# GLA's values by token: two token tiles at a time, placed by transfers within SBUF

## The chip, the cores and the metric

The kernel runs on one core of a Trainium2 chip. The metric is device time in microseconds (us) of one execution, and the median over runs is what is compared. The engines are TensorE (PE, and PEld for its weight loads), VectorE (DVE), ScalarE (ACT), GpSimd (POOL) and SyncE (SP, which here only issues transfers). Each engine works through its own list of instructions in order and waits on semaphores of the others.

## The reference

A two-layer trunk for 512 tokens of width 1024. Layer 0 has one input projection, whose columns feed gated linear attention (GLA, 4 heads, key width 64, value width 128, chunks of 64 tokens) and an RWKV-7 mixer (8 heads of 64); then an output projection, a LayerNorm and a SwiGLU feed-forward. Layer 1 is a latent attention with 16 heads, and another feed-forward. The part that the change touches is the GLA values `v`:

```python
p = x @ w_in                                  # (512 tokens) x (columns)
gq, gk, gv, gg, glr = jnp.split(p_gla, GLA_OFFSETS, axis=-1)
# per chunk of 64 tokens and head, S the state (64 x 128):
o_inter = einsum('bhck,bhkv->bhcv', qi * exp(b), state)
o_intra = einsum('bhij,bhjv->bhiv', attn, vi)
new_state = exp(b_last) * state + einsum('bhck,bhcv->bhkv', ki * exp(b_last - b), vi)
```

Both products take a chunk's values with the 64 tokens on the partitions and the 128 value columns along the free axis.

## The kernel before

Every large product is done in three passes over float32 split in two parts: a rounded part h and a rest l (`gemm3`, lines 184 to 187: three matmuls of 512 columns that accumulate in one PSUM bank). The input x stands in SBUF transposed, as `xh` and `xl` (128 partitions, 8 blocks of 128 rows of x, 512 tokens).

**Weights of layer 0's input projection.** `w_even` lies in HBM as 27 tiles of 128 columns, each with 1024 floats per partition (8 blocks k of 128 columns). `half_w(..., add=True)` (lines 207 to 219) brings half of such a tile, 128 x 512 floats, 256 KB, with 2 KB per partition in one piece:

1. SP issues the transfer into `w` (line 212).
2. ACT writes -w into `wl` (line 214).
3. POOL issues a second transfer of the same weights, which adds them in float32 onto `wl` (line 215); so `wl` becomes what rounding takes away.
4. ACT casts `w` to `wh` (line 216).

`w`, `wh` and `wl` have three buffers each, so a fourth load waits until the first one's products are done. `proj(i)` (lines 251 to 260) takes two such halves for one tile of 128 columns and does 24 matmuls, 12 for each half, with the weights as the stationary side; its result has the columns on the partitions and the tokens along the free axis. The results go to two PSUM banks with the tag "g".

**The values before.** Tiles 19 to 22 are the four heads' values. `plain` (line 830) runs `proj` for each and copies the result to `gv`, column by token. `gla_states` (line 877), for each of the two pairs of heads i, needs them token by column. So `turn` (line 886) multiplies each 128 x 64 piece with the identity: as a matmul for one head (line 891) and as a transpose for the other (line 889), four chunks of both heads into the one PSUM bank with the tag "l"; ACT and DVE copy that bank to `SV` (line 913). There are four such rounds (2 pairs x 2 halves of the chunks). The keys `ke` are turned in the same way ahead of it. Line 919 forms the keys' and values' products, line 927 the states, and `gla_out` (line 955) the outputs.

**The order.** `weave` interleaves the streams (the projections "0 1 2 k 3 v g", four RWKV heads' pairs, GLA, the output projection) by costs in the program, and the framework's scheduler then sets the final order on every engine. So between a projection's products stand small products of the RWKV and GLA streams: lines 870 (GLA scores), 674 and 694 (inversion), 715 (chunk products, 64 x 64), 562, 520. The pool "S2" has 14 buffers of 128 x 512 floats; the `SV` tiles come from it and take those that RWKV's third pair of heads gives back.

Of the kernel before, what the change touches and what calls it, by code (L numbers as in the profile page):

```python
# [17 lines left out]
P = 128  # L18
# [3 lines left out]
CH = 64  # L22
# [184 lines left out]
def half_w(g, src, tag=None, add=False):  # L207

    nc = g.nc
    w = g.tp.tile([P, 512], F32, tag="w", name="w", bufs=3)  # L210
    h, l = (g.T(tag, n, dt=F32R) if tag else g.tp.tile([P, 512], F32R, tag=n, name=n, bufs=3) for n in ("wh", "wl"))
    nc.sync.dma_start(w, src)
    if add:
        nc.scalar.mul(l, w, -1.0)  # L214
        nc.gpsimd.dma_start(l, src, accum_op=ALU.add)  # L215
    nc.scalar.copy(h, w)  # L216
    if not add:
        nc.gpsimd.tensor_tensor(l, in0=w, in1=h, op=ALU.subtract)
    return h, l
# [6 lines left out]
def even_mixer(g, xh, xl, big, big2):  # L226
# [145 lines left out]
            yield from rproj(int(o))  # L372
        done.add("proj")

    gla = gla_projections(g, L, proj, done)

    def rwkv(i):
        while ("r", i) not in done or i > 2 and f"o{i - 3}" not in done:
# [434 lines left out]
    return L  # L813


def gla_projections(g, L, proj, done):
    nc = g.nc
    T = g.T
    g.v, g.gate = [], []

    def keys():
        for i, e in enumerate(L):
            e.q, e.k = T("L", "gq"), T("L", "gk")
            nc.scalar.mul(e.q, proj(15 + 2 * i), 0.125)
            yield 5 * g.slow
            nc.scalar.copy(e.k, proj(16 + 2 * i))
            yield 5 * g.slow
        done.add("gk")

    def plain(dst, c, name):  # L830
        for i in range(4):
            t = T("L" if name == "gv" else "S1", name)
            nc.scalar.copy(t, proj(c + i))
            dst.append(t)
            yield 5 * g.slow
        done.add(name)

    return {"k": keys(), "v": plain(g.v, 19, "gv"), "g": plain(g.gate, 23, "gg")}


def gla_scores(g, L):
# [35 lines left out]
def gla_states(g, L):  # L877


    nc = g.nc  # L880
    C, T, ps = g.C, g.T, g.ps
    ch = lambda t: t.rearrange("p (c t) -> p c t", t=CH)
    hs = [slice(0, 64), slice(64, 128)]
    g.QA, g.SV = [], []

    def turn(h, o, i, one):

        if h:
            nc.tensor.transpose(out=o, in_=i, identity=one)
        else:  # L890
            nc.tensor.matmul(o, lhsT=i, rhs=one, start=True, stop=True)  # L891

    for i, e in enumerate(L):
        ke = T("v", "ke")
        nc.vector.tensor_tensor(ch(ke), in0=bc(ch(e.b)[:, :, CH - 1:CH], [P, NCH, CH]), in1=ch(e.b), op=ALU.subtract)
        exp_ln(g, ke, ke, AF.Exp, scale=1.0 / 16)
        nc.vector.tensor_tensor(ke, in0=ke, in1=e.k, op=ALU.mult)
        p = ps("l")
        for c in range(NCH):
            for h in range(2):  # L900
                turn(h, p[hs[1 - h], c * CH:(c + 1) * CH], ke[hs[h], c * CH:(c + 1) * CH], C("ident")[hs[h], hs[h]])
        kt = T("v", "kt", (P, NCH, CH))
        nc.scalar.copy(kt.rearrange("p c t -> p (c t)"), p)
        yield 4
        SV = [[T("S2", "SV", (P, 4, P)) for r in range(2)] for h in range(2)]
        g.SV += SV
        for r in range(2):
            p = ps("l")
            for j in range(4):
                for h in range(2):  # L910
                    turn(h, p[hs[1 - h], j * P:(j + 1) * P], g.v[2 * i + h][:, (4 * r + j) * CH:(4 * r + j + 1) * CH], C("ident"))
            for h in range(2):
                (nc.vector.tensor_copy if h else nc.scalar.copy)(SV[h][r][hs[1 - h]], p[hs[1 - h]].rearrange("p (c v) -> p c v", v=P))
            yield 3
        for r in range(2):
            o = ps("l")
            for c in range(4 * r, min(4 * r + 4, NCH - 1)):
                for h in range(2):
                    nc.tensor.matmul(o[hs[h], c % 4 * P:c % 4 * P + P], lhsT=kt[hs[1 - h], c], rhs=SV[h][r][hs[1 - h], c % 4], start=True, stop=True)
            for c in range(4 * r, min(4 * r + 4, NCH - 1)):  # L920
                for h in range(2):
                    st, nx, kv = SV[h][r][hs[h], c % 4], SV[h][(c + 1) // 4][hs[h], (c + 1) % 4], o[hs[h], c % 4 * P:c % 4 * P + P]
                    if c == 0:
                        nc.gpsimd.memset(st, 0.0)
                        nc.scalar.copy(nx, kv)
                    else:
                        nc.vector.scalar_tensor_tensor(nx, in0=st, scalar=e.el[hs[h], c:c + 1], in1=kv, op0=ALU.mult, op1=ALU.add)
            yield 3
        qe = T("v", "qe")
        exp_ln(g, qe, e.b, AF.Exp, scale=1.0 / 16)  # L930
        for h in range(2):
            qa = T("S2", "QA", (P, NCH, CH))
            g.QA.append(qa)
            nc.gpsimd.tensor_tensor(qa.rearrange("p c t -> p (c t)")[hs[h]], in0=qe[hs[h]], in1=e.q[hs[h]], op=ALU.mult)
            nc.gpsimd.tensor_copy(qa[hs[1 - h]].rearrange("p c t -> p (c t)"), g.acc[i][hs[1 - h]])
        yield 2
# [886 lines left out]
```

## Time and profile before

| | us |
|---|---|
| median of 3 runs | 1387.27 |
| lowest and highest | 1384.99 and 1394.15 |
| the profiled execution | 1391.69 |
| its span, first to last instruction | 1389.6 |
| PE busy in the span | 1342.3 (97%) |

The page gives the busy time of each engine, the chain that ended last and groups of instructions by line; the trace can be asked for a stretch, a line, or the instructions in order of time. Matmuls overlap in the records: one of 512 columns is shown as 390 ns and the next starts 230 ns after it. So what a matmul takes of PE's time is read from the starts. The granted clock of TensorE stands as a share of 2.4 GHz: 1.00 is 2.4 GHz and 0.50 is 1.2 GHz.

### The profile page before, as it was taken

What the parts mean: (1) busy time and instruction counts of PE and PEld (TensorE: products, weight loads), DVE (VectorE), ACT (ScalarE), POOL (GpSimd) and SP (SyncE); (2) the same over time, 40 slices, a digit from 0 to 9 for tenths busy, and PEclk for the clock granted to TensorE, in tenths of its full rate; (3) what the DMA queues carried; (4) which work ended last, traced back from release to release, by engine and by line L of the source; (5) the groups of instructions that cost most, each with busy time, mean ns of one, the idle gap of its engine ahead of it and who ended that gap; (6) DMA issues with size and microseconds to landing.
All of it is one profiled execution on the core that took longest, in us unless ns stands there. A gap on an engine that the chain in (4) does not pass through costs nothing.

```text
span 1389.6 us, 21744 instructions
## 1 busy us (share of the span) xinstructions
PE 1342.3 (97%) x8382; PEld 1063.7 (77%) x8382; DVE 921.3 (66%) x1704; ACT 685.1 (49%) x1212; POOL 232.6 (17%) x278
## 2 busy tenths in 40 slices
PE   8899999999999899999999999999999899999997
PEld 6577777766678688998888877666677788997886
DVE  3687677644497666668456367988786766667456
ACT  6653344354536455555334356555445455555341
POOL 2230012122311111126401130000011111120000
PEclk9999999979999999999999999999999999999999
DMA  8563343530468788673325422111277787773232
GB/s 244 111 128 59 70 100 68 113 67 32 157 214 191 163 186 166 149 141 84 103 96 149 118 79 58 55 56 46 92 206 172 161 187 167 145 127 93 91 107 90
DMA packets 74328, 168.15 MB, mean 121 GB/s; under 512 B 21232, under 2 KB 22384, under 8 KB 74096
## 3 DMA queue, kind: packets, MB, share of 16 engines
q0 software_dynamic: 21888, 60.83, 26.2%
q1 hardware_dynamic: 51808, 103.83, 22.9%
q10 hardware_dynamic: 528, 2.10, 0.4%
q8 instruction: 66, 1.08, 0.3%
q14 instruction: 38, 0.31, 0.1%
HBM read 163.77 MB, written 2.95 MB: 120 GB/s over the span
## 4 chain that ended last, share of the span: by engine, by line
PE 62%; issue 14%; DMA 10%; DVE 7%; ACT 3%; POOL 2%; SPq 1%; POOLq 0%; DVEq 0%; ACTq 0%
PE ps_g L1239 12%; PE ps_g L186 10%; PE ps_g L187 10%; PE ps_g L185 10%; DMA raw<-in_w_gu 6%; PE ps_s L1624 3%; PE ps_o L1653 2%; PE ps_c L715 2%; PE ps_t L1640 1%; POOL raw L1266 1%; PE ps_c L674 1%; DMA wl<-in_w_even 1%; PE ps_l L891 1%; PE ps_s L1317 1%; PE ps_c L187 1%
## 5 line engine op out<-in xcount | busy, mean ns | idle before, releaser
L192 DVE TENSOR_TENSOR wl<-raw,wh 128x1024 fp32r<-128x1024 f32 (+1 forms) x120 | 132.7, 1114 | 80.2 <-ACT wh L191 79.8
L191 ACT CAST wh<-raw 128x1024 fp32r<-128x1024 f32 (+1 forms) x120 | 116.0, 968 | 138.2 <-PE ps_g L1239 101.1
L1266 POOL DMA_DIRECT2D raw<-in_w_gu x96 | 83.1, 866 | 494.3 <-DVE wl L192 388.5
L1239 PE MATMUL ps_g<-wh,xh 128*128 128x512 f32 (+1 forms) x320 | 118.9, 372 | 2.0 <-ACT wh L191 2.0
L1239 PE MATMUL ps_g<-wh,xl 128*128 128x512 f32 (+1 forms) x320 | 117.8, 368 | 0.0
L187 PE MATMUL ps_g<-xh,wl 128*128 128x512 f32 (+2 forms) x296 | 113.7, 385 | 3.0 <-DMA wl<-in_w_even 1.8
L185 PE MATMUL ps_g<-xh,wh 128*128 128x512 f32 (+2 forms) x296 | 115.6, 391 | 0.0
L186 PE MATMUL ps_g<-xl,wh 128*128 128x512 f32 (+2 forms) x296 | 114.1, 385 | 0.0
L186 PE MATMUL ps_g<-wl,ah 128*128 128x512 f32 x288 | 112.0, 390 | 0.6 <-DVE wl L192 0.6
L185 PE MATMUL ps_g<-wh,ah 128*128 128x512 f32 x288 | 111.7, 392 | 0.6 <-ACT ah L191 0.4
L187 PE MATMUL ps_g<-wh,al 128*128 128x512 f32 x288 | 110.8, 389 | 0.0
L192 DVE TENSOR_TENSOR wl<-w,wh 128x1024 fp32r<-128x1024 f32 (+2 forms) x79 | 89.4, 1131 | 32.0 <-ACT wh L191 31.6
L191 ACT CAST wh<-w 128x1024 fp32r<-128x1024 f32 (+2 forms) x79 | 76.2, 965 | 60.2 <-PE ps_g L186 36.6
L191 ACT CAST ah<-hid 128x512 fp32r<-128x512 f32 x72 | 43.5, 618 | 98.9 <-PE ps_g L186 98.9
L1239 PE MATMUL ps_g<-wh,Sh 128*128 128x512 f32 (+1 forms) x240 | 90.1, 376 | 0.0
L192 DVE TENSOR_TENSOR al<-hid,ah 128x512 fp32r<-128x512 f32 x72 | 49.2, 695 | 60.9 <-ACT ah L191 60.8
L1239 PE MATMUL ps_g<-wh,Sl 128*128 128x512 f32 (+1 forms) x240 | 89.3, 373 | 0.0
L1239 PE MATMUL ps_g<-wl,xh 128*128 128x512 f32 (+1 forms) x320 | 79.7, 371 | 0.9 <-DVE wl L192 0.9
L215 POOL DMA_DIRECT2D wl<-in_w_even x48 | 41.5, 865 | 229.9 <-ACT wl L214 194.8
L216 ACT CAST wh<-w 128x512 fp32r<-128x512 f32 x64 | 39.3, 617 | 81.5 <-PE ps_g L186 49.7
L1239 PEld LDWEIGHTS ps_g<-wh,xh 128*128 128x128 f32 x320 | 60.1, 188 | 10.5 <-ACT wh L191 2.9
L187 PEld LDWEIGHTS ps_g<-xh,wl 128*128 128x128 f32 (+1 forms) x296 | 56.2, 190 | 14.7 <-DMA wl<-in_w_even 3.0
(461 smaller groups left out, 3269.4 us busy)
## 6 DMA issues: line engine op xcount, KB each, us to landing
raw<-in_w_gu POOLq DMA_DIRECT2D x64, 512.0 KB, 5.7
w<-in_w_dn SPq DMA_DIRECT2D x44, 512.0 KB
raw<-in_w_gu SPq DMA_DIRECT2D x32, 512.0 KB
w<-in_w_even SPq DMA_DIRECT2D x48, 256.0 KB
wl<-in_w_even POOLq DMA_DIRECT2D x48, 256.0 KB, 4.7
raw<-in_w_gu POOLq DMA_DIRECT2D x32, 384.0 KB, 4.8
w<-in_w_gu SPq DMA_DIRECT2D x12, 512.0 KB
raw<-in_w_gu SPq DMA_DIRECT2D x16, 384.0 KB
```

The lines of the kernel that those rows point to most:

```text
L185: nc.tensor.matmul(out, lhsT=wh, rhs=xh, start=first, stop=False)
L186: nc.tensor.matmul(out, lhsT=wh, rhs=xl, start=False, stop=False)
L187: nc.tensor.matmul(out, lhsT=wl, rhs=xh, start=False, stop=last)
L191: c = nc.scalar.copy(h, src)
L192: (eng or nc.vector).tensor_tensor(l, in0=src, in1=h, op=ALU.subtract)
L215: nc.gpsimd.dma_start(l, src, accum_op=ALU.add)
L216: nc.scalar.copy(h, w)
L715: nc.tensor.matmul(q[:, CH:] if m else q[:, :CH], lhsT=l, rhs=r, start=m < 2, stop=m != 1)
L1239: nc.tensor.matmul(acc[u][:, :n], lhsT=A_[a][:, k, P * u:P * u + P], rhs=w[:, q], start=first and k + a + b == 0, stop=k + b == 4, skip_gr ...
L1266: nc.gpsimd.dma_start(T[k][k2], w[r, q, k2], accum_op=ALU.add)
L1624: nc.tensor.matmul(p[:, :nk], lhsT=Q[:, h % 4, qb * P:(qb + 1) * P], rhs=K[:, h % 4, :nk], start=True, stop=True)
L1653: nc.tensor.matmul(o[64 * e:64 * e + 64, kb * P:], lhsT=Vv[:, kb, (h - 1 + e) * 64:(h + e) * 64], rhs=t[e][kb][:, kb * P:], start=kb == 0, ...
```

## The change

The values are computed with the tokens on the partitions: the stationary side is now a block of x (128 tokens), the moving side the weights of all four heads, 512 columns. One load brings block k of the four tiles 19 to 22, that is 4 pieces of 512 bytes per partition, which lie 512 KB apart in HBM. Two tiles of tokens are done at a time, in both "g" banks, so each load serves 6 matmuls, and all loads are made twice (two halves of the tokens). The turning products, their bank and their copies are gone; 32 transfers issued by SP, each 64 partitions x 512 bytes, put the values from `gv` into `SV`.

```diff
@@ half_w
+    as_src = lambda t: t.rearrange("p (i c) -> p i c", c=P) if len(src.shape) == 3 else t
-    nc.sync.dma_start(w, src)
+    nc.sync.dma_start(as_src(w), src)
     if add:
         nc.scalar.mul(l, w, -1.0)
-        nc.gpsimd.dma_start(l, src, accum_op=ALU.add)
+        nc.gpsimd.dma_start(as_src(l), src, accum_op=ALU.add)
@@ gla_projections
+    def values():
+
+        for half in range(2):
+            o = [g.ps("g") for u in range(2)]
+            for k in range(NK):
+                h, l = half_w(g, g.I["w_even"][19:23, :, k * P:k * P + P].transpose([1, 0, 2]), add=True)
+                for u in range(2):
+                    ts_ = slice((2 * half + u) * P, (2 * half + u) * P + P)
+                    gemm3(nc, o[u], xh[:, k, ts_], xl[:, k, ts_], h, l, k == 0, k == NK - 1)
+            for u in range(2):
+                g.v.append(T("L", "gv"))
+                nc.scalar.copy(g.v[-1], o[u])
+            yield 10 * g.slow
+        done.add("gv")
+
-    return {"k": keys(), "v": plain(g.v, 19, "gv"), "g": plain(g.gate, 23, "gg")}
+    return {"k": keys(), "v": values(), "g": plain(g.gate, 23, "gg")}
@@ gla_states
-        for r in range(2):
-            p = ps("l")
-            for j in range(4):
-                for h in range(2):
-                    turn(h, p[hs[1 - h], j * P:(j + 1) * P], g.v[2 * i + h][:, (4 * r + j) * CH:(4 * r + j + 1) * CH], C("ident"))
+        for t in range(4):
             for h in range(2):
-                (nc.vector.tensor_copy if h else nc.scalar.copy)(SV[h][r][hs[1 - h]], p[hs[1 - h]].rearrange("p (c v) -> p c v", v=P))
-            yield 3
+                hd, q = 2 * i + h, 2 * (t % 2)
+                for par in range(2):
+                    nc.sync.dma_start(SV[h][t // 2][hs[1 - h], q + par], g.v[t][hs[par], hd * P:hd * P + P])
```

What stands where on the engines changes at three places. A row is the line, the operation, what is written and what is read, with buffer numbers; in the changed program a line of `half_w` is one higher, and one of `gla_states` 13 to 14 higher.

**PE, in the first half of the values.** `ps_g` is the bank; `wh` and `wl` are one load's two parts. Before, the second load of the first head's values:

```order
L185 MATMUL ps_g_2580<-xh_62,wh_2574 128x512
L186 MATMUL ps_g_2580<-xl_63,wh_2574 128x512
L187 MATMUL ps_g_2580<-xh_62,wl_2575 128x512
L185 MATMUL ps_g_2580<-xh_62,wh_2574 128x512
L186 MATMUL ps_g_2580<-xl_63,wh_2574 128x512
L187 MATMUL ps_g_2580<-xh_62,wl_2575 128x512
```

And in the change, the fifth load and the beginning of the sixth:

```order
L185 MATMUL ps_g_2565<-wh_2620,xh_62 128x512
L185 MATMUL ps_g_2566<-wh_2620,xh_62 128x512
L521 MATMUL ps_c3_2686<-sq_2684,cst_60 128x512
L186 MATMUL ps_g_2565<-wl_2621,xh_62 128x512
L187 MATMUL ps_g_2565<-wh_2620,xl_63 128x512
L186 MATMUL ps_g_2566<-wl_2621,xh_62 128x512
L187 MATMUL ps_g_2566<-wh_2620,xl_63 128x512
L185 MATMUL ps_g_2565<-wh_2633,xh_62 128x512
```

The two banks take turns, a load is used up after six products, and the second of them already reads `wl`. Here the scheduler has put both products that read `wh` alone, and one of another stream, ahead of the first that reads `wl`.

**PE, where GLA's states begin.** `ps_l` is the single bank "l". Before, one of the four rounds of turning, with the products around it:

```order
L603 MATMUL ps_c3_2890<-Vt_2828,Mak_2763 64x64 x16
L891 MATMUL ps_l_3445<-cst_60,gv_2565 64x128
L889 MATMUL ps_l_3445<-cst_60,gv_2787 64x128
L891 MATMUL ps_l_3445<-cst_60,gv_2565 64x128
L889 MATMUL ps_l_3445<-cst_60,gv_2787 64x128
L891 MATMUL ps_l_3445<-cst_60,gv_2565 64x128
L889 MATMUL ps_l_3445<-cst_60,gv_2787 64x128
L891 MATMUL ps_l_3445<-cst_60,gv_2565 64x128
L889 MATMUL ps_l_3445<-cst_60,gv_2787 64x128
L187 MATMUL ps_g_3530<-xh_62,wl_3518 128x512
```

Now:

```order
L905 MATMUL ps_l_3442<-cst_60,ke_3438 64x64
L185 MATMUL ps_g_3611<-xh_62,wh_3598 128x512
L186 MATMUL ps_g_3611<-xl_63,wh_3598 128x512
L187 MATMUL ps_g_3611<-xh_62,wl_3599 128x512
L185 MATMUL ps_g_3611<-xh_62,wh_3598 128x512
L186 MATMUL ps_g_3611<-xl_63,wh_3598 128x512
L932 MATMUL ps_l_3517<-SV_3497,kt_3459 64x128
L932 MATMUL ps_l_3517<-SV_3499,kt_3459 64x128
```

The keys are still turned (L905), and the first products that read `SV` follow five products of a gate projection later.

**SP, at the end of the projections.** `do`, `Dc` and `Dct` belong to the inversion of the last RWKV pair. Before:

```order
L635 DMA do_3013<-T16_2914 64x256
L635 DMA do_3023<-T16t_2915 64x256
L212 DMA w_3702<-in_w_even 128x512
L637 DMA Dc_3011<-do_3013 16x8x16 x8
L637 DMA Dct_3012<-do_3023 16x8x16 x8
L212 DMA w_3763<-in_w_eo 128x512
```

Now:

```order
L636 DMA do_3110<-T16_2942 64x256
L927 DMA SV_3639<-gv_2671 64x128 x2
L636 DMA do_3120<-T16t_2943 64x256
L927 DMA SV_3637<-gv_2673 64x128
L638 DMA Dc_3108<-do_3110 16x8x16 x8
L638 DMA Dct_3109<-do_3120 16x8x16 x8
L927 DMA SV_3637<-gv_2673 64x128
L927 DMA SV_3639<-gv_2673 64x128 x2
L927 DMA SV_3638<-gv_3095 64x128 x2
L927 DMA SV_3640<-gv_3095 64x128 x2
L927 DMA SV_3638<-gv_3097 64x128 x2
L927 DMA SV_3640<-gv_3097 64x128 x2
```

Three of the new transfers stand between `do` and `Dc`, and the last load of the gates (`w_3746`) has come to stand behind all of them.

## Rows read from the trace of the kernel before

**Rows 1.** The page, busy time of each engine (share of the span) and instructions.

```profile
PE 1342.3 (97%) x8382; PEld 1063.7 (77%) x8382; DVE 921.3 (66%) x1704; ACT 685.1 (49%) x1212; POOL 232.6 (17%) x278
```

**Rows 2.** By windows, PE alone: us, PE busy (instructions), granted clock, DMA share, GB/s.

```profile
228.00:264.50 36.50, 36.18 (x372) 1.00 0.54 105
279.00:290.00 11.00, 11.00 (x63) 0.50 0.38 60
```

**Rows 3.** PE in order of time: start us, us, line, operation, out<-in, forms.

```profile
255.31 0.39 PE L185 MATMUL ps_g<-xh,wh 128*128 128x512 f32 x1
255.54 0.40 PE L186 MATMUL ps_g<-xl,wh 128*128 128x512 f32 x1
```

**Rows 4.** PE in order of time, rounds of turning values: first rows and successors.

```profile
280.96 0.69 PE L891 MATMUL ps_l<-cst,gv 128*64 128x128 f32 x2
...
284.57 0.77 PE L187 MATMUL ps_g<-xh,wl 128*128 128x512 f32 x1
...
311.48 0.69 PE L891 MATMUL ps_l<-cst,gv 128*64 128x128 f32 x2
...
314.66 0.48 PE L186 MATMUL ps_g<-xl,wh 128*128 128x512 f32 x1
...
317.05 0.43 PE L891 MATMUL ps_l<-cst,gv 128*64 128x128 f32 x2
...
319.42 1.15 PE L674 MATMUL ps_c<-rT,big 64*64 64x64 f32 x32
```

**Rows 5.** Line 215: ns min/median/max; who waited for it (us, times); landing.

```profile
L215 POOL DMA_DIRECT2D wl<-in_w_even x48: 853/862/1007, 15.8 to 307.9; - x48
  PEld ps_g L187: 3.0, 3
DMA to landing us min/median/max: 3.9/4.7/9.5
```

**Rows 6.** ACT in order of time, 241 us: the negated copy of one load.

```profile
241.33 0.63 ACT L214 ACTIVATE wl<-w 128x512 fp32r<-128x512 f32 x1
```

**Rows 7.** POOL in order of time: the same load's adding transfer, and its idle before.

```profile
242.25 0.86 POOL L215 DMA_DIRECT2D wl<-in_w_even  x1 [4.05 <-ACT wl L214]
```

**Rows 8.** The chain that ended last, in order of time: small products between projections.

```profile
226.64 1.15 PE ps_l L870 x32
...
235.60 0.87 PE ps_c L520 x2
...
253.50 1.54 PE ps_c L715 x48
...
257.33 1.09 PE ps_c L562 x16
```

**Rows 9.** Queue of POOL's transfers, 0 to 400 us, then 420 to 460: packets, MB, share.

```profile
q0 software_dynamic: 6912, 12.59, 20.1%
...
q0 software_dynamic: 1019, 3.68, 50.4%
```

**Rows 10.** The page, groups of line 1266: busy us, mean ns, idle before.

```profile
L1266 POOL DMA_DIRECT2D raw<-in_w_gu x96 | 83.1, 866 | 494.3 <-DVE wl L192 388.5
```

**Rows 11.** By windows, all engines: columns PE, PEld, DVE, ACT, POOL, clock, DMA, GB/s.

```profile
52.50:55.00 2.50, 0.00 (x0) 0.00 (x0) 1.25 (x2) 2.50 (x6) 0.00 (x0) 0.90 0.11 20
55.00:60.00 5.00, 4.86 (x10) 3.17 (x11) 3.43 (x7) 4.38 (x10) 1.72 (x2) 0.50 0.57 114
```

**Rows 12.** Groups by line, 0 to 400 us: the negated copies: xcount, busy us, mean ns.

```profile
L214 ACT ACTIVATE wl<-w 128x512 fp32r<-128x512 f32 x48 | 30.0, 625 | 4.4 <-PE ps_g L187 2.5 <-DMA w<-in_w_even 1.8
```

**Rows 13.** Line 913, the copies out of the turning bank: ns min/median/max.

```profile
L913 ACT COPY SV<-ps_l x4: 580/580/582, 285.0 to 319.5; 64x512 f32<-64x512 f32 x4
```

**Rows 14.** Line 637 on SP's queue: issue ns min/median/max.

```profile
L637 SPq DMA_DIRECT2D Dc<-do x32: 331/429/496, 98.9 to 283.5; - x32
```

**Rows 15.** SP's queue in order of time: the last loads of weights for the projections.

```profile
279.67 0.33 SPq L212 DMA_DIRECT2D w<-in_w_even  x1
```

More of the change, by code (lines that the diff above doesn't have):

```diff
@@ L373, in gemms @@
         done.add("proj")
-    gla = gla_projections(g, L, proj, done)
+    gla = gla_projections(g, L, proj, done, xh, xl)
     def rwkv(i):
@@ L813, in gla_begin, with gla_projections @@
     return L
-def gla_projections(g, L, proj, done):
+def gla_projections(g, L, proj, done, xh, xl):
     nc = g.nc
```

## The prediction

> **What bounds the kernel now.** I read the page's busy times first: PE is busy for 97% of the span [rows 1], so what PE does and what it waits for sets the time. Then the stretch in which the values are projected, 228.0 to 264.5 us: PE is busy for 36.18 of 36.5 us at a granted clock of 1.00 (2.4 GHz), and the 16 DMA engines for 0.54 of it [rows 2]. So PE hides all loads there, by a margin that has to be found. Two products of 512 columns start 0.23 us apart [rows 3], though each is shown as 0.39 us; 12 of them, what one load serves, are 2.76 us of PE. Last, the load itself: PE's weight port waits three times for the landing of a `wl`, 3.0 us in all [rows 5]. So the adding transfer is the part of a load that comes last, and it is already late now and then.
>
> **What goes.** The values' own products stay: 96 of 512 columns before (4 heads x 24), and 2 halves x 8 loads x 6 = 96 now. Nothing is won there. The four rounds of turning go. From its first product to the product behind it, a round takes 284.57 - 280.96 = 3.61 us, 314.66 - 311.48 = 3.18 us and 319.42 - 317.05 = 2.37 us [rows 4]. The first runs wholly at half clock (from 279 to 290 us the granted clock is 0.50, that is 1.2 GHz [rows 2]), the last at full. The round I don't show begins at half and ends at full clock, like the 3.18 one; I take 3.0. Sum 12.2 us. At the fast rate throughout it would be 4 x 2.37 = 9.5, at the slow one 4 x 3.61 = 14.4. All of it is on the path, since PE has nothing else to wait for there. The copies out of the bank (four on ACT of 0.58 us [rows 13], four on DVE) count nothing: PE fills their time with gate projections.
>
> The half clock may end earlier. In those 11 us, 3.6 + 0.9 are turning (a first round, and a quarter of the second); the other 6.5 would cost 3.2 less at full clock. But the keys are still turned just ahead of it, so I take 0 and keep 3.2 as an end.
>
> **What comes: loads.** Each load now serves 6 products, 6 x 0.23 = 1.38 us of PE, and there are 16 for the values in place of 8. A load can start when the third one before it is used up (three buffers), and PE can use it a time L later. L now: ACT begins the negated copy at 241.33 [rows 6] and POOL starts the transfer at 242.25 [rows 7], 0.92 us; it lands 4.7 us after that [rows 5]; and ACT comes to it some 0.4 us after the buffers are free (an estimate, from ACT instructions of 0.63 us [rows 12] that may be under way). L = 6.0.
>
> Before, a load of 2.76 us with other streams' products between them had a cover of two loads, 5.5 us, and more. Now the cover is two loads of 1.38 us and what stands between. I went through the changed order load by load with this rule. The other work between is made of blocks of the GLA scores (L870) and of L674 and L694, 1.1 us each; L520, 0.87; L715, 1.54; L562, 1.09 [rows 8]. Added to 22 us of values that is 39.3 us without a wait, like the 36.5 of today. In the first half, most of the other work stands within loads 1 and 2. Load 1 is used up 4.8 us before PE comes to load 4, so PE waits L - 4.8 there; load 2 was used up 2.0 us later than load 1's pace allows, so load 5 waits 2.0; load 7 waits L - 5.7 and load 8, which follows the late load 5, 2.9. In the second half the 715 and 562 blocks cover more: at L = 6.0 the waits are 3.8 us, in all 10.3.
>
> What do pieces of 512 bytes do to L? No row has such an adding transfer. **Lower end:** only bytes count, L = 6.0, waits 10.3. **Packets:** from 0 to 400 us, 20.1% of 16 engines over 6912 packets is 186 ns a packet of 1.82 KB; from 420 to 460 us, 50.4% over 1019 is 316 ns for 3.61 KB [rows 9]. A line through both has 73 ns per KB and 53 ns a packet. Four times the packets (528 with those that signal, for 144) at the same bytes then make 2.9 us on 16 engines out of 1.67: L rises by 1.3 to 7.3, waits 15.6. **Upper end:** POOL's issue takes 0.86 us with 128 rows of 2 KB and 0.87 us with 128 rows of 4 KB [rows 5, 10], so it doesn't follow bytes. If it follows the number of pieces, it becomes 3.4 us, L rises by another 2.6 to 9.9, waits 28.6. I take L = 8.0, the packets and about a quarter of the last, because pieces that POOL has written can move while it writes the others: waits 3.2 + 2.0 + 2.3 + 2.9 for loads 4, 5, 7 and 8, and 8.7 in the second half, 19.1 us.
>
> The Trainium skill (DMA: Bandwidth & Descriptors, Specifications) gives 512 bytes as the smallest transfer at line rate, and its section on one DMA's anatomy calls descriptor generation small; by these L stays at 6.0. The Trainium skill (Perfetto Trace Analysis, DMA Optimizations) says that transfers under 2 KB carry a large overhead each; by that L rises. The sum goes by the rows above.
>
> Waits of PE have a second price: after 2.5 us with PE empty, its clock was granted at 0.50 over the next 5 us [rows 11]. A load's six products at half clock still fit into a wait, so I take 0 and add 3 us at the upper end.
>
> **What comes: other queues.** ACT gets 8 more negated copies and casts, 8 x 1.25 = 10 us, POOL 8 x 0.86; both have idle time between loads (POOL 4.05 us ahead of the one shown [rows 7]), so 0 besides L. SP gets 32 transfers; at the 0.33 to 0.43 us of its small ones [rows 14] that is 11 to 14 us. Behind all of them stands the last load of the gates. Today it is issued at 279.67 us [rows 15] and the last negated copy is added to at 307.9 us [rows 5], so 28 us of cover are there for 14: 0. Without that cover it would be up to 5 us on the last gate. Three transfers stand between `do` and `Dc` of the last RWKV pair: 1.3 us at most; gate products cover it, 0.
>
> **Sum.** -12.2 + 19.1 = +7 us. The profiled execution took 1391.69 us, so 1398.7 there; it was 4.4 us above the median of 1387.27. On the median: **1394 us**.
>
> **Rivals.** *The loads stay hidden* (faster or nothing): L = 6.0, since only bytes count, and the clock recovers early. -12.2 - 3.2 + 10.3 = -5, and with all turning at its slow price -7: 1380 to 1387. For it: the DMA engines are idle 46% of the stretch. Against it: even today PE waits for `wl` at times with twice the products per load, and in the changed order the scheduler itself pulls both products on `wh` and another stream's ahead of the first on `wl`. Chance 0.22; a quarter of it, with a gain elsewhere (the "l" bank, no longer passed through four rounds, lets GLA end earlier), ends over 1% faster.
>
> *POOL writes pieces, not rows* (slower): its issue grows beyond 2 us; L is 9 or more. 24 to 28.6 of waits, less 9.5 to 12.2, and up to 3 for the clock: +12 to +22, 1399 to 1409. It decides from L = 8.9 on, where the sum passes +11.5 us with the clock's price on top. For it: issue is independent of bytes. Against: nothing here shows a POOL issue over 1.01 us. Chance 0.25.
>
> *SP holds up the gates or the inversion*: the sum of the forecast plus 5 to 6, 1400. Against: SP's idle time. Chance 0.06.
>
> *The change doesn't do what it says* (the turning goes, but the scheduler fills every wait with other streams' products, so only the sum of work counts): -12, 1375. Against: PE takes its list in order, and that list has the six products of a load together. Chance 0.04.
>
> **How the numbers follow.** The forecast (L from 6.7 to 8.9, +1 to +11, and up to +14 with the clock) has 0.43. 1% is 13.9 us, about what a measurement of this kernel can tell from no change: below 1373.4 counts as faster, above 1401.1 as slower. Faster: a quarter of 0.22 and some of the 0.04, 0.08. Slower: four fifths of 0.25, half of 0.06, and the upper fifth of the forecast, with the clock's price on it, 0.32. Same: 0.60. The range reaches from the first rival, -9 with the run-to-run difference, to POOL's upper end, +22 and 2 for that: 1378 to 1411. The forecast's own range is 1386 to 1403.
>
> **What would show it.** Right: no L889 and L891 with values; POOL's adding transfers for the values land 1 to 3 us later than now; PE waits for `wl` while it projects values, about 19 us, at the fourth, seventh and eighth load of the first half above all; the stretch of the values grows from 36.5 to about 58 us. Wrong: landing times as now and waits under 10 us (first rival), POOL's issue several times 0.86 us (second), or PE waiting for gates' `w` or for `Dct` (third). What would make the sum itself wrong is a different clock in the stretch, since every product in it then counts double.

## The result and the profile after

The changed kernel takes 1402.54 us (median; 1398.42 to 1406.45), the kernel before 1389.53 us beside it (1384.99 to 1394.15). The ratio is 1.0092, 95% interval 1.0063 to 1.0122: 12.8 us slower (8.8 to 17.0), where +7 was forecast. The profiled execution has a span of 1400.2 us. Below, a difference in us is the ratio less one, times the median of the kernel before that was run beside it.

The page of the changed kernel, busy time of each engine, answers to [rows 1]: PE works 11 us less and waits more, and POOL has the eight loads more.

```profile
PE 1331.3 (95%) x8334; PEld 1057.5 (76%) x8334; DVE 924.1 (66%) x1700; ACT 694.0 (50%) x1225; POOL 245.6 (18%) x286
```

The stretch of the values now lies at 219.3 to 272.1 us, 52.8 us long where it had 36.5 [rows 2]. By windows, PE alone (us, PE busy, granted clock, DMA share, GB/s), and behind it the stretch that was at half clock before:

```profile
219.00:273.00 54.00, 45.79 (x471) 0.91 0.89 156
...
276.00:290.00 14.00, 14.00 (x120) 0.88 0.41 104
```

PE is empty for 8.2 of the 54 us. It was empty for 0.3 us in [rows 2], at a clock of 1.00. The waits of PE in the same stretch (us in total, times, longest) give the reason:

```profile
PE ps_g L186 <- DMA wl<-in_w_even: 7.5, 4, 3.0
```

PE in order of time at three of the four waits (start us, us, line, operation, out<-in, idle before it and what ended it):

```profile
236.51 0.50 PE L186 MATMUL ps_g<-wl,xh 128*128 128x512 f32 x1 [2.99 <-DMA wl<-in_w_even]
...
239.37 0.80 PE L186 MATMUL ps_g<-wl,xh 128*128 128x512 f32 x1 [1.13 <-DMA wl<-in_w_even]
239.96 0.63 PE L187 MATMUL ps_g<-wh,xl 128*128 128x512 f32 x1
240.38 0.63 PE L185 MATMUL ps_g<-wh,xh 128*128 128x512 f32 x1
...
258.24 0.79 PE L186 MATMUL ps_g<-wl,xh 128*128 128x512 f32 x1 [2.32 <-DMA wl<-in_w_even]
```

Load 5 comes 3.0 us late and load 6 1.1 us; in the second half load 11 comes 1.1 us late and load 12 2.3 us. The other twelve loads are in time. From 239.96 us on, products start 0.43 us apart, where 0.23 is the full rate [rows 3]: the granted clock has fallen. It does so once more behind the wait at 256 us. By windows (columns PE, PEld, DVE, ACT, POOL, clock, DMA share, GB/s):

```profile
235.00:240.00 5.00, 2.36 (x7) 1.41 (x8) 0.00 (x0) 1.67 (x3) 1.08 (x1) 0.75 1.06 169
240.00:245.00 5.00, 5.00 (x15) 3.71 (x13) 1.12 (x2) 2.91 (x5) 1.55 (x3) 0.57 0.69 124
...
255.00:260.00 5.00, 2.68 (x9) 1.88 (x8) 1.23 (x4) 1.14 (x2) 1.33 (x2) 0.79 1.27 234
260.00:265.00 5.00, 5.00 (x42) 3.36 (x42) 1.03 (x3) 2.27 (x4) 1.71 (x2) 0.86 0.82 134
```

So the stretch shows two prices: 7.5 us of waits, and 54 x (1 - 0.91) = 4.9 us of clock, a share that counts time in which PE waits too. Read from the starts, 19 products run at half clock and take some 8.6 us where 19 x 0.23 are 4.4. But over 219 to 290 us the mean granted clock is 0.90 in both kernels, since the one before loses as much behind the stretch [rows 2]; whether the two losses belong together isn't shown.

What holds the loads back is the buffer. ACT's waits in the stretch, and its negated copies for loads 5, 6 and 12, in order of time:

```profile
ACT wl L215 <- PE ps_g L186: 17.3, 10, 4.4
```

```profile
229.29 0.63 ACT L215 ACTIVATE wl<-w 128x512 fp32r<-128x512 f32 x1 [0.53 <-PE ps_g L186]
...
230.66 0.63 ACT L215 ACTIVATE wl<-w 128x512 fp32r<-128x512 f32 x1 [0.23 <-PE ps_g L186]
...
249.34 0.63 ACT L215 ACTIVATE wl<-w 128x512 fp32r<-128x512 f32 x1 [0.88 <-PE ps_g L186]
```

The copy begins when PE has done the last product that reads the buffer's former load, and PE's first product that reads the new `wl` follows 7.2, 8.7 and 8.9 us later. The adding transfer itself, line 216 (was 215), 14 of the 16, from 214 to 262 us: ns of issue min/median/max, and the time to landing. In [rows 5] the issue was 862 ns; in the kernel before, the same line had landings of 4.0/4.4/5.0 from 200 to 275 us.

```profile
L216 POOL DMA_DIRECT2D wl<-in_w_even x14: 1273/1282/1301, 214.4 to 261.3; - x14
...
DMA to landing us min/median/max: 4.3/5.8/8.3
```

SP's transfers into `SV`, ns of issue min/median/max, and SP's queue behind the values, in order of time:

```profile
L927 SPq DMA_DIRECT2D SV<-gv x32: 461/594/1280, 246.4 to 310.3; - x32
```

```profile
290.42 0.46 SPq L636 DMA_DIRECT2D do<-T  x1
290.92 1.24 SPq L927 DMA_DIRECT2D SV<-gv  x2
292.60 0.46 SPq L636 DMA_DIRECT2D do<-T16t  x1
293.11 0.59 SPq L927 DMA_DIRECT2D SV<-gv  x1
293.80 4.84 SPq L638 DMA_DIRECT2D Dc<-do  x8
299.03 4.93 SPq L638 DMA_DIRECT2D Dct<-do  x8
...
310.96 0.54 SPq L213 DMA_DIRECT2D w<-in_w_even  x1
```

From the first `do` to the end of the last `Dct` issue it is 13.5 us. The first row of `do` in the kernel before stands at 276.46 and the end of its last `Dct` at 287.84: 11.4 us.

### The profile page after: what moved, and what is told of

Same layout as the page of the kernel before. It is cut to its first block, busy times and chain, and to the rows that moved or that the text cites. A ratio compares the mean times of both kernels' runs of the same rounds, so it can differ in the third digit from the quotient of the medians.

```text
span 1400.2 us, 21755 instructions
## 1 busy us (share of the span) xinstructions
PE 1331.3 (95%) x8334; PEld 1057.5 (76%) x8334; DVE 924.1 (66%) x1700; ACT 694.0 (50%) x1225; POOL 245.6 (18%) x286
## 4 chain that ended last, share of the span: by engine, by line
PE 53%; issue 19%; DMA 13%; DVE 7%; ACT 3%; POOL 3%; SPq 1%; POOLq 0%; DVEq 0%; ACTq 0%
PE ps_g L186 10%; PE ps_g L185 10%; PE ps_g L187 10%; DMA raw<-in_w_gu 8%; PE ps_g L1252 6%; PE ps_s L1637 3%; PE ps_o L1666 2%; DMA wl<-in_w_even 2%; POOL raw L1279 2%; PE ps_c L716 2%; PE ps_t L1653 1%; PE ps_c L675 1%; DMA w<-in_w_even 1%; DVE wl L192 1%; DMA wl<-in_w_mi 1%
## 5 line engine op out<-in xcount | busy, mean ns | idle before, releaser
L187 PE MATMUL ps_g<-xh,wl 128*128 128x512 f32 (+2 forms) x264 | 100.2, 380 | 4.2 <-DMA wl<-in_w_even 3.4
L186 PE MATMUL ps_g<-xl,wh 128*128 128x512 f32 (+2 forms) x264 | 100.4, 380 | 0.0
L185 PE MATMUL ps_g<-xh,wh 128*128 128x512 f32 (+2 forms) x264 | 99.6, 377 | 0.0
L216 POOL DMA_DIRECT2D wl<-in_w_even x56 | 55.1, 984 | 198.7 <-ACT wl L215 159.5
L217 ACT CAST wh<-w 128x512 fp32r<-128x512 f32 x72 | 43.9, 614 | 63.7 <-PE ps_g L186 35.5
L1252 PEld LDWEIGHTS ps_g<-wl,xh 128*128 128x128 f32 x320 | 58.0, 188 | 10.2 <-DVE wl L192 2.4
```

The lines of the kernel that those rows point to most:

```text
L185: nc.tensor.matmul(out, lhsT=wh, rhs=xh, start=first, stop=False)
L186: nc.tensor.matmul(out, lhsT=wh, rhs=xl, start=False, stop=False)
L187: nc.tensor.matmul(out, lhsT=wl, rhs=xh, start=False, stop=last)
L216: nc.gpsimd.dma_start(as_src(l), src, accum_op=ALU.add)
L1252: nc.tensor.matmul(acc[u][:, :n], lhsT=A_[a][:, k, P * u:P * u + P], rhs=w[:, q], start=first and k + a + b == 0, stop=k + b == 4, skip_gr ...
```

## The experiments

Each is timed against the kernel before in three or five rounds. The theories: A, each load is made twice and serves half the products; B, pieces of 512 bytes; C, the transfers on SP's queue; D, no other stream's work stands between the loads.

**A null.** The kernel before, run as if it were a change.

> The kernel before once more, unchanged, as a measure of what no change looks like: ratio 1.000 within 0.003. Its profile tells whether the stretch at half clock at 279 to 290 us is in every execution (theory: it is not; the mean granted clock of an execution, 0.985 to 0.996, goes with its time, some 1394 down to 1380 us) or a fixed part of the program.

Measured: 1.0005 (0.9976 to 1.0033). PE at 276 to 290 us:

```profile
276.00:290.00 14.00, 14.00 (x87) 0.63 0.37 66
```

The half clock is there again, a little later and shorter: the theory that it isn't in every execution found no support in the two profiles. The first addition of the output projection, the end of this part of the program, comes at 384.24 us in one profile and at 388.03 in the other. So a single profile says nothing about differences under 4 us.

**Deeper buffers.**

```diff
-    w = ... bufs=3      -    wh, wl: bufs=3
+    w = ... bufs=2      +    wh: bufs=3, wl: bufs=4
```

> The change with the same nine load buffers shared out otherwise: two for w, three for wh, four for wl, in all projections. Theory A (three wl buffers and loads of only six products set the values' pace): a wl may start one load earlier, so most of the waits for its landing go and the time falls by 6 to 10 us, to 1393 to 1397. Theory B (the pieces of 512 bytes, that is POOL's issue and the packets, are the loss): at 16 loads the DMA engines and POOL set the pace, buffers help 0 to 3 us. Theory C (the 32 transfers into SV hold up SP and the last inversion): no difference, 1402.

Measured: 1.0151 (1.0099 to 1.0202), not faster than the changed kernel. Waits for `wl` fall to 5.2 us; the clock in the stretch doesn't recover:

```profile
219.00:273.00 54.00, 48.41 (x494) 0.91 0.85 153
```

ACT's waits in the stretch say what took over:

```profile
ACT wl L215 <- DMA w<-in_w_even: 13.3, 9, 2.5
```

In the changed kernel ACT's copies wait for PE to give `wl` back (17.3 us in ten waits); here they wait for the landing of `w`, which lost a buffer. So the run moves the limit from one ring of buffers to the next, and doesn't tell what a fourth `wl` beside three `w` would give.

**Whole pieces.** The weights of the values lie in HBM in the order in which the changed kernel wants them, 2 KB per partition.

```diff
+    A["w_gv"] = ...                    # (block k, 128, 4 tiles x 128)
-                h, l = half_w(g, g.I["w_even"][19:23, :, k * P:k * P + P].transpose([1, 0, 2]), add=True)
+                h, l = half_w(g, g.I["w_gv"][k], add=True)
```

> The change with the values' weights laid out so that each of the 16 loads reads 2 KB in one piece per partition; all else the same. Theory A: the time from a freed buffer to a landed wl falls by about 1 us of some 7, the waits shrink by a third, 1396 to 1400. Theory B: the loss goes, POOL's issue is back at 0.86 us, 1388 to 1394. Theory C: no difference, 1402.

Measured: 1.0087 (1.0052 to 1.0121), as the changed kernel. The issue is back at 862 ns and the landing nearly so, yet PE waits as long. The line (217 here), and the waits of PE in the stretch:

```profile
L217 POOL DMA_DIRECT2D wl<-in_w_gv x13: 853/862/871, 216.7 to 256.4; - x13
...
DMA to landing us min/median/max: 3.8/4.6/7.8
```

```profile
PE ps_g L187 <- DMA wl<-in_w_gv: 7.1, 3, 3.8
```

Theory B falls as the main loss: the small pieces cost 1.2 us of landing and 0.42 us of issue, and no time that can be measured; by the two intervals, some 6 us either way can't be excluded. The waits are fewer but longer. This profile is of an execution 6.7 us above the run's median, and its clock in the stretch is 0.84. Another rival falls too, that the 16 DMA engines are full: their share of the stretch, 0.89 in the changed kernel, is 0.69 here, at the same time.

**Making the loads twice, alone.** The kernel before, with its turning.

```diff
+        if 19 <= i < 23:
+            for k in range(NK):
+                if k % 2 == 0:
+                    h, l = half_w(g, g.I["w_even"][i][:, 512 * (k // 4):512 * (k // 4) + 512], add=True)
```

> The kernel before, turning and all, with one thing changed: each load of the values' weights is made twice, and each making feeds six products instead of twelve (16 loads of 2 KB pieces in place of 8, the products and their order the same, the yields between the four projections kept). Theory A (twice the loads on six products each is the whole loss of the change): 10 to 13 us slower than before, ratio 1.007 to 1.0095, with PE waits for the values' wl of 15 us or more between 225 and 270 us. Theory D (the loss comes from the change giving the loads no other work between them: 48 products of one stream in a row, where before has 24 and then other streams): here the other work stands between every four loads, so at most 4 us, ratio up to 1.003, waits for wl under 6 us.

Measured: 1.0094 (1.0061 to 1.0128), +13.1 us (8.5 to 17.8). The waits of PE in the stretch, and windows:

```profile
PE ps_g L187 <- DMA wl<-in_w_even: 6.9, 6, 2.4
```

```profile
219.00:273.00 54.00, 44.63 (x527) 1.00 0.71 147
...
245.00:250.00 5.00, 1.96 (x7) 1.05 (x6) 4.86 (x11) 1.46 (x3) 0.21 (x1) 1.00 0.92 203
...
270.00:275.00 5.00, 2.16 (x8) 1.35 (x8) 4.02 (x19) 0.58 (x1) 0.00 (x0) 0.84 0.65 173
275.00:280.00 5.00, 5.00 (x17) 3.77 (x15) 0.00 (x0) 2.08 (x4) 0.08 (x1) 0.50 0.00 0
```

PE is empty for 9.4 us of the stretch, at a clock of 1.00 (the first row is PE alone, the rest all engines). A seventh wait of 2.8 us, for a load of the gates, lies behind it, in 270 to 275 us, where PE has work for 2.16 us; after it the clock is 0.50. Theory A is shown for the kernel before: this edit alone costs as much as the whole change. Of the waits, less than the expected 15 us are there, 9.8 us with the seventh. In D's own terms, work of other streams between every four loads isn't enough.

**Loads made once.** Two heads at a time, 256 columns, for all four tiles of tokens; a load serves 24 products of 256 columns. Two more products, with zeros, open the two banks for each pair of heads.

```diff
-        for half in range(2):
+        for c in range(2):
...
-            for k in range(NK):
+            for kk in range(NK // 2):
+                h, l = half_w(g, g.I["w_even"][19 + 2 * c:21 + 2 * c, :, kk * 256:kk * 256 + 256].transpose([1, 0, 2]), add=True)
+                for k in (2 * kk, 2 * kk + 1):
+                    for t in range(4):
+                        gemm3(nc, o[t // 2][:, t % 2 * 256:t % 2 * 256 + 256], ...)
```

> The change with the loads made once: two heads (256 columns) at a time for all four token tiles, two token tiles in one bank, so 8 loads as before, each serving 24 products of 256 columns, in pieces of 1 KB. The weight loads of PE double. Theory A: the cover is back to 2.76 us a load, the waits go and the gain of the turning stays, 1380 to 1388, unless PE's weight loads no longer hide under products of 256 columns (then up to 10 us more). Theory B: half the loads, pieces twice as long, also 1382 to 1390. Theory C: 1400.

Measured: 1.0017 (0.9991 to 1.0043). No wait for `wl` is left, and the clock is back; PE in order of time shows products of 256 columns 0.120 us apart, as 0.23 for 512:

```profile
219.00:273.00 54.00, 53.03 (x697) 1.00 0.53 109
```

```profile
235.72 0.28 PE L185 MATMUL ps_g<-wh,xh 128*128 128x256 f32 x1
235.84 0.28 PE L186 MATMUL ps_g<-wl,xh 128*128 128x256 f32 x1
```

With theory A undone, some 10 us of the changed kernel's 12.8 come back, and the turning's gain still doesn't appear.

**Loads made twice, spread.** The changed kernel, giving way to the other streams after each load.

```diff
+                if k < NK - 1:
+                    yield 1.25 * g.slow
...
-            yield 10 * g.slow
+            yield 1.25 * g.slow
```

> The changed kernel with the yields of the values spread: after each load's six products the other streams get a turn (1.25 instead of 10 at the half's end), so that scores and chunks of the other mixer stand between the loads; number of loads, products and transfers as in the changed kernel. Theory D: the loads are then covered and the time falls to 0.998 to 1.003 of before, PE waits for wl under 6 us. Theory A (the doubled traffic itself, whatever stands between): ratio 1.007 to 1.010, as the changed kernel, since DMA and POOL's issue of 1.3 us stay as many. A rival to both: the two accumulators of the half are held longer and the streams that are let in wait for banks; then over 1.010.

Measured: 1.0029 (1.0006 to 1.0053), by the two ratios 8.8 us less than the changed kernel. The same number of loads, and nearly the same waits, but in seven pieces and none over 1.6 us; in all of the stretch, with the windows that were at 0.57 and 0.86, the clock stays at 1.00. The second row of windows goes on to 290 us, and the third is the changed kernel over the same time:

```profile
PE ps_g L186 <- DMA wl<-in_w_even: 6.7, 7, 1.6
```

```profile
219.00:273.00 54.00, 46.56 (x584) 1.00 0.85 148
219.00:290.00 71.00, 62.89 (x692) 0.95 0.79 141
```

```profile
219.00:290.00 71.00, 62.79 (x611) 0.90 0.79 145
```

A in its strict form, the doubled loads whatever stands between them, falls: as many loads cost 8.8 us less. D as put (waits covered) falls too, but its time came true: the waits stay, and the clock's loss in the stretch is gone. As part of it comes back behind the stretch, the clock gives 71 x (0.95 - 0.90) = 3.5 us in these two profiles. The rest of the 8.8 us isn't told apart, and that the clock is the cause rests on one profile of each: in the run with copies below, with the same loads as the changed kernel, the stretch is at 0.87 where it was 0.91.

**The turning's products gone, nothing in their place.** The copies take the values unturned, so `SV` doesn't hold the values by token.

```diff
-            p = ps("l")
-            for j in range(4):
-                for h in range(2):
-                    turn(h, p[hs[1 - h], ...], g.v[2 * i + h][...], C("ident"))
...
-                (...)(SV[h][r][hs[1 - h]], p[hs[1 - h]]...)
+                (...)(SV[h][r][hs[1 - h]], g.v[2 * i + h][hs[1 - h]]...)
```

> The kernel before without the 64 products that turn the values, nothing in their place: the eight copies stay and take the values unturned from SBUF, so what SV holds isn't the values by token. It prices the turning alone. If the turning is on the path for the 12.2 us that its four rounds take: ratio 0.991 to 0.993. If only what the placing run gained (0.9976) is there to gain and its 32 transfers cost nothing: 0.996 to 0.998. If 0.991 to 0.993, the 32 transfers cost some 6 to 9 us of it. The rounds gone, the chain of the other mixer behind them is what is late next: then nothing below 0.996.

Measured: 0.9939 (0.9916 to 0.9962), -8.5 us (5.3 to 11.7). And the kernel before **with the 32 transfers** in place of turning and copies; here the projections still give columns by token, so `SV` again doesn't hold the values by token, and the turns that the copies gave other streams (`yield 3`) are gone too:

```diff
-        for r in range(2):                       # turning and copies
...
+        for t in range(4):
+                for par in range(2):
+                    nc.sync.dma_start(SV[h][t // 2][hs[1 - h], q + par], g.v[t][hs[par], hd * P:hd * P + P])
```

> The kernel before with the turning products and copies taken out and the 32 transfers put in, the projections left as they were (what is placed in SV is then not the turned values: the turn itself is left out). It prices the second half of the change alone. Theory A and B: PE loses 12 us of work and nothing else, 1376 to 1380. Theory C: the transfers cost what they save, 1388 to 1392.

Measured: 0.9976 (0.9949 to 1.0004), -3.3 us. PE at 276 to 290 us, first without the products, then with the transfers:

```profile
276.00:290.00 14.00, 14.00 (x142) 0.88 0.50 95
```

```profile
276.00:290.00 14.00, 14.00 (x150) 1.00 0.39 66
```

Both are above the 0.51 to 0.63 of the kernel before, although the keys are still turned ahead of it. So the turning is worth 8.5 us, and the 32 transfers would take 5 of them back. That difference is at the edge of what two intervals can tell, and the part of the program ends at 371.00 and 371.88 us in the two profiles, so this pair doesn't show where.

**Copies in place of the transfers**, in the changed kernel.

```diff
-                    nc.sync.dma_start(SV[h][t // 2][hs[1 - h], q + par], g.v[t][hs[par], hd * P:hd * P + P])
+                    (nc.vector.tensor_copy if h else nc.scalar.copy)(SV[h][t // 2][hs[1 - h], q + par], g.v[t][hs[par], hd * P:hd * P + P])
```

> The changed kernel with one part put back: the 32 transfers within SBUF are 32 copies (16 on ACT, 16 on DVE, 64 x 128 each, half of them across partitions); loads and projections as in the changed kernel. The kernel without the turning's products came to 0.9939 and the one with the 32 transfers in their place to 0.9976, so the transfers may cost 5 us (0 to 10). Theory C (they do, by SP's queue): 1.003 to 1.006 here. Theory A alone (the doubled loads are all that costs, the transfers nothing): 1.008 to 1.010, as the changed kernel. Rival: ACT and DVE have 4 to 5 us more each right where the states begin, and both stand in the chain there: 1.010 or more.

Measured: 1.0044 (1.0024 to 1.0065), by the two ratios 6.7 us less than the changed kernel, whose interval just meets this one. The waits for `wl` are the same there (7.1 us in four), so the loads explain none of it. SP's queue:

```profile
292.59 0.45 SPq L636 DMA_DIRECT2D do<-T  x1
...
298.25 3.80 SPq L638 DMA_DIRECT2D Dct<-do  x8
```

The inversion's way over SP takes 9.5 us here against 13.5: it begins 2.2 us later and ends 1.9 us earlier. But what it feeds doesn't come earlier on PE by that. The inversion makes five groups of products on L675; the first and the fourth, in the changed kernel first, with copies second:

```profile
310.38 0.97 PE L675 MATMUL ps_c<-kT,big 64*64 64x64 f32 x26
...
322.25 1.55 PE L675 MATMUL ps_c<-kT,big 64*64 64x64 f32 x32 [3.25 <-DVE rT L683]
```

```profile
313.27 1.15 PE L675 MATMUL ps_c<-kT,big 64*64 64x64 f32 x32
...
322.38 1.15 PE L675 MATMUL ps_c<-kT,big 64*64 64x64 f32 x32 [0.35 <-DVE rT L683]
```

The first group comes 2.9 us earlier with the transfers than with copies. Neither profile shows a wait for `Dc` or `Dct`, and the chain that ended last in the changed kernel holds no transfer from 285 to 330 us. The lead is lost ahead of the fourth group, where PE waits 3.25 us for DVE, and DVE's instruction ahead of the awaited one, line 777, took 2.73 us. Why it took so long isn't shown.

So a price of the transfers is supported by two pairs of runs (5.2 and 6.7 us), each at the edge of its intervals. Theory C's way, the inversion held up on SP's queue, isn't borne out by the trace. The last gates' load is issued at 310.96 us with the transfers and before 285 with copies, but no product of a gate waits for it.

**The values straight from PSUM to their place**, loads made once; then the same, spread.

```diff
-                nc.scalar.copy(g.v[t][:, c * 256:c * 256 + 256], o[t // 2][...])
+                for h in range(2):
+                    for par in range(2):
+                        (nc.vector.tensor_copy if h else nc.scalar.copy)(g.V4[2 * c + h][t // 2][hs[1 - h], 2 * (t % 2) + par], o[t // 2][hs[par], ...])
```

> Two heads at a time for all four tiles of tokens with the loads made once (that came to 1.0017 with the transfers), and the values go from PSUM straight to their place in SV: 32 copies of 64 x 128 on ACT and DVE take the place of the copies to gv and of the 32 transfers. Products of 256 columns cost 1.2 us more than those of 512 (192 x 0.120 against 96 x 0.2275 us) and the opening ones 0.9. If turning is worth 8.5 us (the run without its products) and nothing else comes: 0.994 to 0.997. If the transfers had been free: as before that, 1.000 to 1.003. Rival: the 16 copies on DVE lie in the stretch of the values, where DVE carries the other mixer's chain, or the eight SV tiles, held from 245 us on instead of 280, leave others without a slot: over 1.003.

> As the run with the values straight from PSUM, and the other streams get a turn after each load's 24 products (2.5 instead of 10 at the end of the two heads). Theory A: nothing waits for loads there, so spreading gives nothing: within 0.003 of the run without it. Theory D (a stream given way to earlier is worth something in itself, as spreading gave 9 us to the changed kernel, more than the 8 us of PE waits that are left in it): 0.003 to 0.006 faster than the run without it. Rival: accumulators held longer keep the gates' projections and the other mixer out of the two banks: slower by up to 0.005.

Measured: 1.0101 (1.0072 to 1.0130), and 1.0038 (1.0016 to 1.0060) spread. The rival named beforehand, tiles held early, won in the first, by a way that I hadn't seen. POOL in order of time:

```profile
245.25 1.19 POOL L216 DMA_DIRECT2D wl<-in_w_even  x1 [2.10 <-ACT wl L215]
255.59 0.20 POOL L941 MEMSET SV<- 64x128 f32 x1 [9.14 <-PE ps_c L716]
287.98 0.20 POOL L941 MEMSET SV<- 64x128 f32 x1 [32.19 <-PE ps_c L716]
295.59 1.21 POOL L216 DMA_DIRECT2D wl<-in_w_even  x1 [7.41 <-ACT wl L215]
```

The states' zeroing stands on POOL in front of the gates' loads and waits 9 and 32 us for the third RWKV pair to give the buffer back. From 250 to 290 us no load moves (DMA share 0.01 and 0.05), and PE is busy for 26.7 of 40 us. Spreading puts it less far ahead (22.95 us of wait).

**What the runs point to**: loads made once, spread, and copies for transfers.

```diff
+                if kk < NK // 2 - 1:
+                    yield 2.5 * g.slow
...
-                    nc.sync.dma_start(SV[h][t // 2][hs[1 - h], q + par], ...)
+                    (nc.vector.tensor_copy if h else nc.scalar.copy)(SV[h][t // 2][hs[1 - h], q + par], ...)
```

> The parts that the runs so far favour, together: loads made once (two heads at a time for all four tiles of tokens), the other streams let in after each load's 24 products, and 32 copies of ACT and DVE in place of the 32 transfers. The run with once-made loads and transfers came to 1.0017; copies for transfers took 0.0048 from the changed kernel; spreading is taken at 0 to 0.003 where nothing waits for loads. Sum: 0.994 to 0.997, faster than both kernels. Rival: the copies' 4 to 5 us on each of DVE and ACT show once no wait for loads hides them: 0.998 to 1.002.

Measured: 1380.93 us against 1387.57, ratio 0.9948 (0.9924 to 0.9971): faster than both kernels, by 7.2 us than the one before. In the stretch PE is as full as before, and no wait for `wl` is left:

```profile
219.00:273.00 54.00, 52.73 (x740) 1.00 0.48 94
```

It keeps most of what the turning was worth (-8.5 us). Copies and spreading came in together, so the run doesn't tell what each gave.

## Why the prediction was right, and where its terms were off, point by point

**The whole.** Slower by more than nothing and less than 1% was forecast, and that came, at 12.8 us instead of 7. Three terms were off, partly against each other. As measured apart they are -8.5 (turning), +13.1 (loads) and +5 to +7 (transfers), 10 to 12 in all. That the sum came out within 6 us is in part luck: the loads were taken 6 us too high, and the turning's gain and the transfers together 9 to 11 too favourably.

**Turning, -12.2, of which the runs show 8.5.** The rounds were read in the one profile, and the first of them lay wholly at half clock [rows 4]. The end of "the fast rate throughout", 9.5, is the nearer. That the half clock "may end earlier", priced at 0 with an end of -3.2, did happen: 0.88 and 1.00 at 276 to 290 us in the runs without turning, 0.88 in the changed kernel. That it ended because the turning went isn't shown: with the turning kept and the loads made twice it is 0.85 there.

**Loads, +19.1.** The mechanism was right: a load waits for the third one before it, PE waits for `wl`, and the stretch grows, to 52.8 us (58 predicted). Which loads and how long was wrong. Waits were predicted for loads 4, 5, 7 and 8, and 8.7 us in the second half. Loads 4, 7 and 8 didn't wait, loads 5 and 6 did, and the second half waited 3.4 us: 7.5 in all, where the sign of being right said about 19. L was taken as 8.0. With the median landing of 5.8 it is 0.92 + 0.4 + 5.8 = 7.1, the packets' term alone: +1.4 on the landing of 4.4 where +1.3 was worked out. For loads 5, 6 and 12, which PE waited for, it was more: 7.2 to 8.9 us from the copy to the product in the rows above, with landings of up to 8.3; POOL issued loads 5 to 7 within 4.1 us. So one L for all loads was the wrong form. The part of POOL's issue was too much: four times the pieces made it 1.28 us, not 3.4, and that lies within the landing. At L = 7.1 the rule gives about 15 us of waits, and 7.5 of waits with 4 to 5 of clock, some 12, were measured. And most of the loss isn't in the pieces: with whole ones, the median L is 0.92 + 0.4 + 4.6 = 5.9, and the time is the same within some 6 us.

The Trainium skill (Perfetto Trace Analysis, DMA Optimizations) ascribes a significant overhead per transfer to those under 2 KB. Read for the 512-byte pieces of one transfer, the run with whole pieces shows that overhead as 1.2 us of landing, and shows no time for it.

**The waits' second price, the clock, taken as 0, with 3 at the upper end.** The thought behind it, that "six products at half clock still fit into a wait", is what the trace shows for load 7 and the start of load 8: they run at half clock and don't wait. But the clock's share is a price in the stretch all the same, 4 to 5 us: spread waits of nearly the same sum leave the clock there at 1.00 and the kernel 8.8 us faster. Why the clock falls behind some waits and not behind others stays open: where loads are made twice in the kernel before, PE is busy for 1.96 of the 5 us from 245 us on, and the clock stays at 1.00.

**"Three transfers stand between `do` and `Dc` ... 0", and nothing for the rest of the 32.** As a price, this term was mis-sized: put back as copies, the transfers give 6.7 us, and in the kernel before they take 5.2. Each takes SP 0.46 to 1.28 us (median 0.594), not 0.33 to 0.43 [rows 14], and the way of the inversion over SP, with slower issues of `Dc` too, is 2.2 us longer than before and 4.1 longer than with copies. But it isn't shown that the time pays for this way: the two profiles show no engine that waits for it, and in two other runs that have the transfers, the kernel before with them and the spread loads, it takes 11.4 and 11.7 us, about as before. By which way they cost 5 to 7 us stays open. The cover of the last gates' load was enough, as predicted.

**Rivals.** Loads that stay hidden: the landing rose and PE waits. POOL writing pieces: the issue grew by half, not beyond 2 us. The scheduler filling the waits: no. SP holding up the gates or the inversion, the forecast plus 5 to 6, 1400 us: in time this is the nearest to what happened, and it had a chance of 0.06; its way, a wait for `Dct` or for the gates' `w`, isn't in the trace.

**Open.** By which way the transfers cost time; what a fourth `wl` beside three `w` would give; and how the 8.8 us of spreading divide.

## What to carry to other kernels

Count what each load serves before anything else: halving the products per load cost 13 us here with nothing else changed, more than the whole work that the new layout saved. Then look at what stands between the loads: the same doubled loads cost 8.8 us less when other work was spread between them. Don't take small transfers within SBUF as free because their queue has idle time: here 32 of them cost 5 to 7 us, and copies on ACT and DVE were the better mover. Before a wait is blamed on a longer way, compare the same step in both traces: here the way was longer and the step came earlier. When a buffer is taken earlier, look for the instruction that now waits for it, and at what stands behind that one on its engine.

## What the runs showed of the hardware that was not expected

An adding transfer of the same 256 KB takes POOL 0.86 us to issue in 128 pieces of 2 KB, 1.19 us in 256 of 1 KB and 1.28 us in 512 of 512 bytes: it follows neither bytes nor pieces in proportion. Seven waits of at most 1.6 us, 6.7 us in all, left the granted clock at 1.00, and four with 7.5 us, the longest 3.0, were followed by stretches at 0.57 and 0.86. The longest wait alone doesn't decide it: the fall to 0.86 came behind one of 2.3 us, while with the loads made twice in the kernel before six waits with 6.9 us, the longest 2.4, left the clock at 1.00, and a seventh of 2.8 us was followed by 0.50. A transfer within SBUF of 64 x 512 bytes took SP 0.594 us at the median.
